# A hybrid DeltaNet and S5 layer: S5 setup, gate sums and chunk decays placed differently

## The chip, the cores and the metric

One core of one Trainium2 chip runs the program. The metric is the device time of that core in microseconds (us), the median of several executions. The engines are TensorE (PE in the rows, its weight load PEld), VectorE (DVE), ScalarE (ACT), GpSimd (POOL) and SyncE (SP, which here only issues DMAs). TensorE accumulates in PSUM; everything else lives in SBUF or in DRAM.

## What is computed

One layer of a streaming encoder: 4096 prompt frames and 32 sample frames of width 1024 go through an RMSNorm and one input projection. Its columns feed a gated DeltaNet (4 heads of 128) and an S5 state-space group (32 groups of 16 channels), each with a SiLU gate path; both outputs are joined, projected and added to x, and a last RMSNorm follows. Cut to what matters here:

```
q, k, v = silu(causal_conv4(h @ W_qkv));  q = l2norm(q) / sqrt(128);  k = l2norm(k)
beta = sigmoid(b);  g = -exp(A_log) * softplus(a + dt_bias);  gc = cumsum(g) in a block
decay = tril(exp(gc_i - gc_j))
lower = strict_tril((beta k) @ k.T * decay) + I
u = lower^-1 (beta v);  w = lower^-1 (beta k exp(gc));  attn = tril(q @ k.T * decay)
v_new = u - w @ S
o = (q * exp(gc)) @ S + attn @ v_new
S = S * exp(gc_last) + (k * exp(gc_last - gc)).T @ v_new
o_dn = rms_norm(o) * silu(z_dn)
S5: x_t = Lbar x_{t-1} + Bbar u_t;  y = Re(C x_t) + D u_t;  gy = gelu(y)
o_s5 = gy * sigmoid(gy @ glu_w + glu_b) * silu(z_s5)
x_new = x + concat(o_dn, o_s5) @ W_out;  y = rms_norm(x_new)
```

## The kernel before

The order of the instructions of each engine is fixed when the program is built, by a planner with estimated durations; an engine runs its own list in order and waits at its head. Products that need precision are three fp16 products of split operands: `pair` and `split` write a high half (ScalarE) and a low half (VectorE or GpSimd), `mm3` multiplies them.

**Stage one** (`phase_a`, up to about 640 us) normalises x, projects u for the S5 blocks (`uproj`), runs the S5 blocks and fills TensorE with the gate projections (`zproj`). `prep0` and `wfull` bring the first input and weights; `s5_setup` (L594) then makes the constants: exponentials, sines and powers of a 128x16 tile by short VectorE instructions, the rotation tables `rc` and `rs_` by doubling (L791 to L803), the B, C and Toeplitz matrices. It runs after the first projections, in the stretch 62 to 184 us. `s5_block` ends each group with eight stores of gy (L911) on SP. `gates` (L919) makes the decay sums `gc` and beta of all 32 prompt chunks, stores gc, exp(gc) and beta to DRAM (L976, L979), and transposes two of them on TensorE. `phase_b1` follows: it loads gc back (`gcr`), and `table` (L1004) makes from it, chunk by chunk, the decay matrix `dm` and stores it.

**Stage two** (`phase_b`, 922 to about 2086 us) interleaves on TensorE one dense stream (the projections of q, k, v and the S5 gate output, L48 with tile `pp`) with four streams of chunks of 128 frames. `Drive` orders them: a stream that yields n comes back when TensorE's own reckoned time has gone on by 1.5 n, and the chunk with the lowest number goes first. There are 33 chunks: 32 of the prompt and one for the sample. Chunk k uses the tiles of stream k mod 4, so tiles named `br`, `gr`, `knT`, `vb`, `kn` of chunk k are used again by chunk k+4.

A chunk (`chunk`, L1453) first loads exp(gc) into `gr` and beta into `br` (both spread over all partitions). **Front:** k's rows are transposed and squared, the root `rk` of the square sum is taken (`rsqrt`, L125: a power on GpSimd, L129, then three VectorE steps, L130 to L132), `kn` = k·rk; `br` is multiplied by the decay `dm` on GpSimd (L1548), q by `gr` (L1550) and split; the products k kᵀ and k qᵀ follow, and `at` in the tile of `br` (L1560). **Inverse** (`inverse`, L1639): on one of two slots, blocks of 4, 8, 16, 32 and 64 are inverted in a chain TensorE to VectorE and back (L1681, L1696, L1700, L1714, L1728), with a final correction (L1742 to L1746); its result U lies in the tile of `br` too. **Tail:** in the order of the chunks, the state `S` is split into `sp`, R and `vn` are made, `po` gets q·exp(gc)·S and attn·v_new (six products a head in one PSUM tile), `pS` updates S (L1614). Then the squares of `po`, the root `ro`, the gate z and the output (L1630) follow, split into `m16` (in the tile of `dm`) and stored by GpSimd (L1636). `load_dm` brings the decay matrix of a later chunk on SP (L1449).

**The last part** (2086 to 2454 us) is the output projection (`out`).

Of the kernel before, what the change touches and what calls it, by code (L numbers as in the profile page):

```python
# [6 lines left out]
F32 = mybir.dt.float32  # L7
# [10 lines left out]
H = 4  # L18
# [61 lines left out]
class Trunk:  # L80
    def __init__(self, ctx, tc, io, T):
# [6 lines left out]
        self.ws, self.un, self.uz, self.marks = {}, {}, {}, []  # L88
# [6 lines left out]
        self.ones = self.pool(self.ones_pool, "a_one").tile([128, 128], F32, name="ones")  # L95
# [6 lines left out]
        nc.vector.tensor_copy(self.ident16, self.ident)  # L102
        self.h_d = [self.dram.tile([2, 1024, 1024], F16, name=f"h_d{b}") for b in range(T // 1024)]
# [130 lines left out]
    def phase_a(self):  # L234
# [26 lines left out]
        nc.gpsimd.memset(self.rowo, 1.0)  # L261
        with ExitStack() as sc:
# [6 lines left out]
            self.un["zd"] = self.wfull(stg, "zd", self.w_z, self.nw, [mk[i] for i in w0], [mk[i] for i in w1], name="xz")  # L269
# [19 lines left out]
        self.s5_setup(tb)  # L289
# [54 lines left out]

        self.gcr = {key: self.tbl.tile([128, 128], F32, name="gc" + key, bufs=1)[:n] for key, n in (("p", H * self.NC), ("s", H))}
        for key, t in self.gcr.items():
            nc.sync.dma_start(t, self.gc_d[key].rearrange("h c t -> (h c) t"))
        order = list(range(self.NC))
        order.insert(2 * SP, self.NC)
        with self.tc.high_priority(offset=-250):  # L350
            for ci in order:
                self.table(ci)
        self.phase_b1()
# [25 lines left out]
    def wload(self, pool, nm, k0, k1, name="xw"):  # L379
# [69 lines left out]
    def h_hl(self, x, p):  # L449
# [3 lines left out]
        nc.sync.dma_start(xn, x)  # L453
# [140 lines left out]
    def s5_setup(self, wt):  # L594
        tc, nc, io = self.tc, self.nc, self.io
# [8 lines left out]
        self.wo8 = wt.tile([128, G, 8, 16], F32, name="wo8")  # L604
        with ExitStack() as sc:
            st = self.pool(sc, "a_s", side="right")

            def t16(nm):
                return st.tile([128, 16], F32, name=nm)

# [1304 lines left out]
```

## Time and profile before

| | |
|---|---|
| median of 3 runs | 2460.18 us (2457.91 to 2461.07) |
| the profiled execution | 2456.1 us, span of the trace 2454.4 us |
| TensorE busy | 2080.0 us, 85% |
| VectorE, ScalarE, GpSimd busy | 1578.9, 1204.6, 892.4 us |

The trace is of one execution. A share of busy time is an average over stages with different limits, so the rows below are by stretch, by line and by wait. A wait is put down to the engine or DMA whose end came last.

### The profile page before, as it was taken

Reading aid. Unit: us, or ns where it says so; the run is one execution under the profiler, and the core shown is the slowest. Engines: PE = TensorE matmul, PEld = TensorE weight load, DVE = VectorE, ACT = ScalarE, POOL = GpSimd, SP = SyncE. Lnnn points to the kernel's source line nnn. Section 1 sums busy time; section 2 is a strip of 40 time slices with the busy share of each in tenths; the row PEclk is TensorE's granted clock in tenths of the full one; section 3 lists DMA queues with packets and bytes.
Section 4 is the critical chain, followed back from the end, with each engine's and each line's share of the span. In section 5 each row is a group of like instructions: output and inputs, shape, how many; then the busy total and the mean of one; then the engine's idle time right before and its main releaser. Section 6 shows DMA issues by size and latency. Waiting matters only on the chain.

```text
span 2454.4 us, 47429 instructions
## 1 busy us (share of the span) xinstructions
PE 2080.0 (85%) x18040; PEld 1491.3 (61%) x18040; DVE 1578.9 (64%) x3715; ACT 1204.6 (49%) x3518; POOL 892.4 (36%) x1057
## 2 busy tenths in 40 slices
PE   3968898967799996986988789888878866999998
PEld 2635676734576554875777677777677743554443
DVE  3885766756474224886888778887878786642222
ACT  5457456423593113656666566666656564421101
POOL 1363011011102014556555555655655455420000
PEclk9989999979899997998999999999999888999999
DMA  5469877367864555231342233333333256455552
GB/s 164 152 165 248 164 164 183 67 75 104 233 174 125 116 123 112 57 80 40 79 83 69 62 66 85 76 83 76 62 58 58 58 143 123 117 142 155 152 146 90
DMA packets 458005, 278.05 MB, mean 113 GB/s; under 512 B 345112, under 2 KB 412928, under 8 KB 457264
## 3 DMA queue, kind: packets, MB, share of 16 engines
q1 hardware_dynamic: 435024, 206.94, 40.0%
q0 software_dynamic: 18000, 59.43, 7.3%
q10 hardware_dynamic: 4752, 8.65, 1.0%
q8 instruction: 141, 2.31, 0.4%
q14 instruction: 88, 0.72, 0.1%
HBM read 110.99 MB, written 86.23 MB: 80 GB/s over the span
## 4 chain that ended last, share of the span: by engine, by line
PE 32%; DVE 22%; DMA 15%; issue 14%; POOL 7%; ACT 6%; SPq 3%; POOLq 0%; DVEq 0%; ACTq 0%
PE pp L48 17%; PE pz L503 7%; DMA br<-be_d 6%; PE bk L48 4%; DVE acc L1354 3%; DMA gyt<-gy_d 2%; DMA h_d<-hl 2%; SPq L911 1%; DVE ubd L1687 1%; DMA gy_d<-vv 1%; DVE vv L879 1%; POOL br L1548 1%; PE bk L52 1%; PE pp L511 1%; DVE vv L885 1%
## 5 line engine op out<-in xcount | busy, mean ns | idle before, releaser
L503 PE MATMUL pz<-wz,hz 128*128 128x512 f16 (+1 forms) x1464 | 383.2, 388 | 20.3 <-DMA hz<-h_d 13.2
L1354 DVE SCALAR_TENSOR_TENSOR acc<-pp,cwu,acc 128x256 f32<-128x256 f32 x540 | 253.0, 475 | 39.1 <-ACT acc L1352 34.8
L48 PEld LDWEIGHTS <-mx 128*128 128x128 f16 (+1 forms) x1584 | 152.7, 98 | 178.8 <-issue 4.3
L503 PEld LDWEIGHTS <-hz 128*128 128x128 f16 (+1 forms) x1464 | 144.3, 100 | 179.2 <-issue 20.7
L48 PE MATMUL pp<-h,wk 128*128 128x259 f16 (+1 forms) x1632 | 224.6, 274 | 0.7 <-DVE gyt L1437 0.4
L48 PE MATMUL pp<-h,wv 128*128 128x259 f16 (+1 forms) x1632 | 220.3, 279 | 1.2 <-DVE acc L1354 1.2
L48 PE MATMUL pp<-h,wq 128*128 128x259 f16 (+1 forms) x1632 | 215.2, 275 | 1.3 <-DVE acc L1354 1.3
L511 PE MATMUL pp<-wa,ht 128*128 128x260 f16 x1536 | 189.8, 279 | 26.0 <-ACT wa L207 11.9
L48 PE MATMUL po<-wo,mx 128*128 128x512 f16 (+1 forms) x912 | 197.2, 379 | 0.3 <-ACT th L1184 0.3
L511 PEld LDWEIGHTS <-ht 128*128 128x128 f16 x1536 | 151.0, 100 | 52.8 <-issue 25.1
L48 PEld LDWEIGHTS <-wk 128*128 128x128 f16 x1632 | 155.1, 99 | 28.6 <-issue 3.6
L48 PEld LDWEIGHTS <-wv 128*128 128x128 f16 x1632 | 151.9, 101 | 33.4 <-issue 9.5
L48 PEld LDWEIGHTS <-wq 128*128 128x128 f16 x1632 | 151.6, 99 | 31.1 <-issue 9.5
L48 PE MATMUL pp<-wo,mx 128*128 128x512 f16 x672 | 153.9, 382 | 0.0
L537 POOL DMA_DIRECT2D z_d<-zt x64 | 36.7, 574 | 311.5 <-DVE zt L536 276.6
L48 PEld LDWEIGHTS <-a 128*128 128x128 f16 x1320 | 83.3, 102 | 89.1 <-issue 65.9
L536 DVE SCALAR_TENSOR_TENSOR zt<-zt,pz 128x512 f32<-128x512 f32 (+1 forms) x66 | 45.0, 682 | 134.7 <-ACT zt L535 134.5
L1522 ACT ACTIVATE jk<-bk 128x128 bf16<-128x128 f32 x396 | 109.9, 278 | 44.1 <-PE bk L52 32.5
L1548 POOL TENSOR_TENSOR br<-br,dm 128x512 f32<-128x512 f32 x33 | 42.4, 1284 | 196.9 <-DMA br<-be_d 137.0
L48 PE MATMUL pp<-wg,gh 128*128 128x512 f16 (+1 forms) x396 | 107.7, 403 | 6.0 <-DVE acc L1354 3.4
L1810 ACT ACTIVATE junk<-xt 128x1024 bf16<-128x1024 f32 (+1 forms) x19 | 20.1, 1056 | 176.4 <-issue 92.6
L1352 ACT ACTIVATE acc<-pp,cwu 128x256 f32<-128x256 f32 x180 | 85.1, 476 | 40.0 <-PE pp L48 26.9
(614 smaller groups left out, 4960.8 us busy)
## 6 DMA issues: line engine op xcount, KB each, us to landing
xn<-in_x SPq DMA_DIRECT2D x32, 512.0 KB, 6.0
h_d<-hl POOLq DMA_DIRECT2D x32, 512.0 KB, 5.2
z_d<-zt POOLq DMA_DIRECT2D x64, 256.0 KB, 3.7
xt<-in_x SPq DMA_DIRECT2D x18, 512.0 KB, 4.5
out_y<-xt SPq DMA_DIRECT2D x18, 512.0 KB, 3.6
dm_d<-tdm ACTq DMA_DIRECT2D x33, 256.0 KB, 3.2
dm<-dm_d SPq DMA_DIRECT2D x33, 256.0 KB, 2.8
gy_d<-vv SPq DMA_DIRECT2D x128, 64.0 KB, 2.3
```

What stands on the lines that cost most here:

```text
L48: return self.nc.tensor.matmul(out, lhs, rhs, start=start, stop=stop)
L52: return self.nc.tensor.transpose(out, src, ident)
L503: self.nc.tensor.matmul(ps, a[x][:, c], w[:, y, c], start=c == 0 and x == y == 0, stop=c == K - 1 and x == 1)
L511: self.nc.tensor.matmul(pu[hf][:, :260], ht[x][:, c, :m], self.w_a[:, y, c, 260 * hf:260 * hf + 260], start=c == 0 and x == y == 0, stop=c ...
L536: nc.vector.scalar_tensor_tensor(zt, zt, 1.0, pz, op0=ALU.add, op1=ALU.mult)
L537: nc.gpsimd.dma_start(rows(dst[0][blk]) if blk >= 0 else dst[1], zt)
L879: v.tensor_tensor(vv, vv, rs, op=ALU.mult)
L885: v.tensor_tensor_scan(*(t.rearrange("p a m -> p (a m)") for t in (vv[:, ri], rt, a[:, ri])), 0.0, op0=ALU.mult, op1=ALU.add)
L1352: nc.scalar.activation(acc, ps[:, 0:n], AF.Copy, scale=cw[:, e, 0:1])
L1354: v.scalar_tensor_tensor(acc, ps[:, j:j + n], cw[:, e, j:j + 1], acc, op0=ALU.mult, op1=ALU.add)
L1522: act.activation(junk, src[:, h], AF.Square, accum_out=out[:, h:h + 1])
L1548: gp.tensor_tensor(br, br, dm, op=ALU.mult)
```

## The change

- **Stage one.** `gates` keeps `gc` in the SBUF tile `gcr` from which `table` reads; it is no longer stored and loaded, and exp(gc) is neither made nor stored. exp(gc) per frame (`ngC` after an exponential) is made once after the tables. Stores of gy go out on GpSimd. `s5_setup` becomes a generator: its first part (constants, powers, rotation tables, with tiles in the space of `toep`) runs after the first inputs and weights have been prepared and ahead of the first projections; the rest runs where all of it stood. The loads of the gate weights wait for the fifth load of x.
- **Roots of a chunk.** `rsqrt4` makes the whole root on GpSimd: the power and four short steps, the last scaling folded in; the short sums beside it go to GpSimd as well.
- **Decays out of PSUM.** q is no longer multiplied by exp(gc) ahead of the product. `po` is made twice: first q·S, which ScalarE copies to `oa` (in the tile of `br`) with the factor exp(gc); then attn·v_new, which VectorE adds to `oa`. The output product reads `oa` from SBUF.
- **beta.** One tile `bl` holds beta of the next chunk; its load is issued on SP right after the multiply of the chunk before.
- **Inverse.** `a32` is made on GpSimd, `affine_select` acts on `br` before L1560, two selections go to ScalarE; the correction `e` is made on TensorE, which adds `Tf` and minus the identity into the same PSUM tile.
- `m16` uses the tile of `knT`. q's SiLU is made by ScalarE's own function, as for k and v, with one scaling per block of q.

```diff
+    def rsqrt4(self, x, tag, f):
+        gp = self.nc.gpsimd
...
+        gp.tensor_tensor(y, x, self.mhalf, op=ALU.pow)
+        gp.tensor_tensor(t, y, y, op=ALU.mult)
+        gp.tensor_tensor(t, t, x, op=ALU.mult)
+        gp.tensor_scalar(t, t, -3.0, -0.5 * f if isinstance(f, float) else f, op0=ALU.add, op1=ALU.mult)
+        gp.tensor_tensor(y, y, t, op=ALU.mult)
+        return y
@@ phase_a @@
+        setup = self.s5_setup(tb)
...
             hts += [self.prep0(s) for s in range(1, 8)]
...
-            self.un["zd"] = self.wfull(stg, "zd", self.w_z, self.nw, ..., name="xz")
+            self.un["zd"] = self.wfull(stg, "zd", self.w_z, self.nw, ..., name="xz", mark=self.xloads[4])
+            next(setup)
...
-        self.s5_setup(tb)
+        assert next(setup, None) is None
...
-        self.gcr = {key: self.tbl.tile(...) ...}
-        for key, t in self.gcr.items():
-            nc.sync.dma_start(t, self.gc_d[key].rearrange("h c t -> (h c) t"))
...
+        gcf = self.ngC.rearrange("t h c -> t (h c)")
+        self.last_exp = nc.scalar.activation(gcf, gcf, AF.Exp, scale=-1.0)
@@ s5_block @@
-                nc.sync.dma_start(gy[s], gn[16 * s:16 * s + 16, :, :128])
+                gp.dma_start(gy[s], gn[16 * s:16 * s + 16, :, :128])
@@ gates @@
-                gc = gp.tile([128, 128], F32, name="gc")[:p]
+                gc = self.gcr[key]
...
-                nc.scalar.activation(x, gc, AF.Exp)
-                nc.gpsimd.dma_start(self.eg_d[key].rearrange("h c t -> (h c) t"), x)
...
-                for t, dr, col in ((gc, self.gc_d, self.gcC), (hb, self.be_d, self.hbC)):
-                    nc.gpsimd.dma_start(dr[key].rearrange("h c t -> (h c) t"), t)
+                nc.gpsimd.dma_start(self.be_d[key].rearrange("h c t -> (h c) t"), hb)
+                for t, col in ((gc, self.gcC), (hb, self.hbC)):
@@ qkv @@
-                if b and nm != "q":
+                if b:
                     self.after(nc.scalar.activation(dst[:, h], acc, AF.Silu), self.last_exp)
...
+                    if b and nm == "q":
+                        nc.scalar.activation(dst, dst, AF.Copy, scale=self.sq["p"])
+    def load_be(self, ci):
+        self.bl = self.ck.tile([128, H, 128], F32, name="bl")
+        src = self.be_d["p"][:, ci] if ci < self.NC else self.be_d["s"][:, 0]
+        self.nc.sync.dma_start(self.bl, src.partition_broadcast(128))
@@ chunk @@
-        gr = t4("gr")
-        nc.sync.dma_start(gr, self.eg_d[key][:, cd].partition_broadcast(128))
         br = t4("br")
         dm = self.dms.pop(ci)
-        nc.sync.dma_start(br, self.be_d[key][:, cd].partition_broadcast(128))
...
-        rk = self.rsqrt(sk[:, 0], 128, H, "k")
+        rk = self.rsqrt4(sk[:, 0], "k", 1.0)
...
-        gp.tensor_tensor(br, br, dm, op=ALU.mult)
-        t = tmp()
-        gp.tensor_tensor(t[:, :, :m], qT[:, :, ts], gr[:, :, :m], op=ALU.mult)
-        qe = pair(gr, t)
+        gp.tensor_tensor(br, self.bl, dm, op=ALU.mult)
+        i = self.order.index(ci) + 1
+        if i < len(self.order):
+            self.load_be(self.order[i])
+        gp.affine_select(out=br, in_=br, ..., compare_op=ALU.not_equal, fill=0.0, base=0, channel_multiplier=-1)
...
-        v.tensor_scalar(sk[:, 1], sk[:, 1], self.eq[key], self.tau[key], op0=ALU.add, op1=ALU.mult)
+        gp.tensor_scalar(sk[:, 1], sk[:, 1], self.eq[key], self.tau[key], op0=ALU.add, op1=ALU.mult)
...
+        po = bk(self.po)
+        for h in range(H):
+            mm3(po[:, h], at_(qp, h), at_(sp, h))
         vn = pair(t4("knT"), pvn, v)
+        oa = t4("br")
+        for h in range(H):
+            act.activation(oa[:, h], po[:, h], AF.Copy, scale=self.ngC[:, h, ci:ci + 1])
         yield 2000
         po = bk(self.po)
         for h in range(H):
-            mm3(po[:, h], at_(qe, h), at_(sp, h), stop=False)
-            mm3(po[:, h], at_(aT, h), at_(vn, h), start=False)
+            mm3(po[:, h], at_(aT, h), at_(vn, h))
...
+        v.tensor_tensor(oa, oa, po, op=ALU.add)
-        squares(po, so)
-        v.scalar_tensor_tensor(so, so, 1.0 / 128, sk[:, 1], op0=ALU.mult, op1=ALU.add)
-        ro = self.rsqrt(so, 128, H, "o")
-        v.tensor_scalar(ro, ro, self.sdn, None, op0=ALU.mult)
+        squares(oa, so)
+        gp.tensor_tensor(so, so, sk[:, 1], op=ALU.add)
+        ro = self.rsqrt4(so, "o", self.hdn)
...
-            v.scalar_tensor_tensor(o[:, h], po[:m, h], ro[:m, h:h + 1], zc[:m, h], op0=ALU.mult, op1=ALU.mult)
+            v.scalar_tensor_tensor(o[:, h], oa[:m, h], ro[:m, h:h + 1], zc[:m, h], op0=ALU.mult, op1=ALU.mult)
...
-        m16 = dm.rearrange(...)
+        m16 = t4("knT").rearrange(...)
@@ inverse @@
-        v.tensor_tensor(a32, at, hb(self.bd32), op=ALU.mult)
-        gp.affine_select(out=at, in_=at, ..., compare_op=ALU.not_equal, fill=1.0, base=0, channel_multiplier=-1)
+        gp.tensor_tensor(a32, at, hb(self.bd32), op=ALU.mult)
...
-        v.tensor_scalar(T64[:, :, 32:64], T, self.rsel[:, 1:2], None, op0=ALU.mult)
+        act.activation(T64[:, :, 32:64], T, AF.Copy, scale=self.rsel[:, 1:2])
...
-        v.tensor_scalar(Tf[:, :, 64:128], T64, self.rsel[:, 3:4], None, op0=ALU.mult)
+        act.activation(Tf[:, :, 64:128], T64, AF.Copy, scale=self.rsel[:, 3:4])
...
-            pe.mm(p[:, h], al[:, h], Tf[:, h], start=False, stop=True)
-        e = t4("br")
-        v.scalar_tensor_tensor(e, p, -1.0, hb(self.ident), op0=ALU.mult, op1=ALU.add)
+            pe.mm(p[:, h], al[:, h], Tf[:, h], start=False, stop=False)
+            pe.mm(p[:, h], ident16, Tf[:, h], start=False, stop=False)
+            pe.mm(p[:, h], ident16, self.nid16, start=False, stop=True)
         eh = i4("a4")
-        act.copy(eh, e)
+        act.activation(eh, p, AF.Copy, scale=-1.0)
         el = i4("a32")
-        gp.tensor_tensor(el, e, eh, op=ALU.subtract)
+        v.scalar_tensor_tensor(el, p, -1.0, eh, op0=ALU.mult, op1=ALU.subtract)
```

## Rows read from the trace of the kernel before

**Rows 1.** Stretches: length; PE, PEld, DVE, ACT, POOL busy (x); clock; DMA

```profile
0.00:62.00 62.00, 22.17 (x192) 18.04 (x192) 20.18 (x55) 32.53 (x73) 8.49 (x26) 0.94 0.52 162
62.00:184.00 122.00, 98.12 (x656) 61.31 (x657) 102.92 (x348) 58.58 (x128) 59.27 (x81) 0.90 0.55 159
62.00:640.00 578.00, 463.84 (x3700) 336.47 (x3701) 388.94 (x910) 289.48 (x819) 133.45 (x208) 0.91 0.72 153
982.00:1964.00 982.00, 833.01 (x9275) 709.93 (x9273) 794.10 (x1953) 598.84 (x1906) 560.88 (x586) 0.94 0.31 68
```

**Rows 2.** Waits, whole run: us in all, times, longest us

```profile
POOL br L1548 <- DMA br<-be_d: 137.0, 21, 9.8
...
DVE rqt_k L130 <- POOL rq_k L129: 90.7, 26, 6.2
...
POOL br L1548 <- PE bk L48: 31.5, 6, 8.6
```

**Rows 3.** Timeline of GpSimd, 1500 to 1506 us: start, us, instruction

```profile
1500.47 1.27 POOL L1548 TENSOR_TENSOR br<-br,dm 128x512 f32<-128x512 f32 x1 [5.15 <-DMA br<-be_d]
...
1502.53 0.22 POOL L1525 TENSOR_SCALAR sk<-sk 128x4 f32<-128x4 f32 x1
...
1504.85 1.14 POOL L1483 TENSOR_TENSOR sp<-S_p,sp 128x512 f16<-128x512 f32 x1
```

**Rows 4.** The chain that ended last, by line (part 4 of the page)

```profile
PE pp L48 17%; PE pz L503 7%; DMA br<-be_d 6%; PE bk L48 4%; DVE acc L1354 3%; DMA gyt<-gy_d 2%; DMA h_d<-hl 2%; SPq L911 1%; DVE ubd L1687 1%; DMA gy_d<-vv 1%; DVE vv L879 1%; POOL br L1548 1%; PE bk L52 1%; PE pp L511 1%; DVE vv L885 1%
```

**Rows 5.** Waits of the whole run, TensorE's for the inverse

```profile
PE bk L48 <- DVE T L1681: 30.1, 27, 5.8
PE bk L48 <- DVE T L1700: 29.9, 17, 4.8
...
PE bk L48 <- DVE p L1696: 21.9, 19, 2.9
```

**Rows 6.** VectorE by line and form, 980 to 1964: busy, mean ns

```profile
L1354 DVE SCALAR_TENSOR_TENSOR acc<-pp,cwu,acc 128x256 f32<-128x256 f32 x483 | 225.6, 475 | 18.8 <-ACT acc L1352 15.6
...
L1360 DVE SCALAR_TENSOR_TENSOR qT<-th,acc 128x256 f32<-128x256 f32 x56 | 44.0, 809 | 17.0 <-PE bk L48 8.5 <-PE bk L52 7.2 <-ACT th L1359 1.3
...
L1630 DVE SCALAR_TENSOR_TENSOR kn<-bk,rq_o,vb 128x128 f32<-128x128 f32 x100 | 27.9, 339 | 0.2
...
L1714 DVE TENSOR_SCALAR T<-T,rsel 128x128 f16<-128x128 f16 x28 | 20.7, 740 | 0.0
...
L1560 DVE SCALAR_TENSOR_TENSOR br<-bk,br 128x512 f32<-128x512 f32 x28 | 19.2, 685 | 7.1 <-PE bk L48 6.9
...
L131 DVE TENSOR_TENSOR rqt_k<-rqt_k,sk 128x4 f32<-128x4 f32 x27 | 5.1, 187 | 0.1
```

**Rows 7.** Timeline of TensorE, 1484 to 1490 us

```profile
1485.64 0.83 PE L48 MATMUL bk<-tp,knT 128*128 128x128 f16 x12
```

**Rows 8.** ScalarE's groups by line and form, whole run

```profile
L1538 ACT ACTIVATE vb<-bk,hbC 128x128 f32<-128x128 f32 x132 | 37.8, 371 | 8.2 <-PE bk L52 7.0 <-DVE bk L1497 1.2
```

**Rows 9.** Waits of SP, 980 to 1964 us

```profile
SPq L1449 <- DMA mx_d<-dm: 244.3, 23, 22.2
```

**Rows 10.** Timeline of TensorE, 596 to 632 us

```profile
623.58 5.96 PE L1012 MATMUL pt<-gcp,ident 128*128 128x128 f32 x32 [22.63 <-DMA gcp<-gc_d]
```

**Rows 11.** Timeline of VectorE, 616 to 617 us

```profile
616.46 0.15 DVE L138 TENSOR_SCALAR am_g<-am_g 128x1 f32<-128x1 f32 x1 [22.06 <-POOL am_g L144]
```

**Rows 12.** VectorE's groups by line, 62 to 184 us

```profile
L800 DVE TENSOR_TENSOR rt<-rot_s,rot_c 128x256 f32<-128x256 f32 (+4 forms) x11 | 5.6, 505 | 0.0
...
L799 DVE TENSOR_TENSOR rot_c<-rot_c 128x256 f32<-128x256 f32 (+4 forms) x11 | 3.6, 347 | 0.0
...
L163 DVE SCALAR_TENSOR_TENSOR ea_s<-ea_s,er_s 128x16 f32<-128x16 f32 x15 | 2.6, 174 | 0.1
```

**Rows 13.** The costliest groups (part 5 of the page)

```profile
L537 POOL DMA_DIRECT2D z_d<-zt x64 | 36.7, 574 | 311.5 <-DVE zt L536 276.6
```

**Rows 14.** Waits of the whole run, TensorE's for the state

```profile
PE bk L48 <- ACT sp L1482: 12.7, 5, 3.9
```

More of the change, by code (lines that the diff above doesn't have):

```diff
@@ L94, in __init__ @@
         self.ones_pool = ExitStack()
-        self.ones = self.pool(self.ones_pool, "a_one").tile([128, 128], F32, name="ones")
+        one = self.pool(self.ones_pool, "a_one")
+        self.ones = one.tile([128, 128], F32, name="ones")
+        self.gcr = {key: one.tile([128, 128], F32, name="gc" + key)[:n] for key, n in (("p", H * T // 128), ("s", H))}
         nc.gpsimd.memset(self.ones, 1.0)
@@ L604, in s5_setup, with tile @@
         self.wo8 = wt.tile([128, G, 8, 16], F32, name="wo8")
+        left, made = [self.toep.rearrange("p x g n -> p (x g n)").bitcast(F32), 0], {}
+        class Room:
+            def tile(_, shape, dt, name):
+                if name not in made:
+                    n = 1
+                    for k in shape[1:]:
+                        n *= k
+                    t = left[0][:, left[1]:left[1] + n]
+                    left[1] += n
+                    made[name] = t.rearrange("p (a k) -> p a k", a=shape[1]) if len(shape) == 3 else t
+                return made[name]
@@ new lines, in s5_setup, with t16 @@
+        st = Room()
+        def t16(nm):
+            return st.tile([128, 16], F32, name=nm)
+        are, aim, ldt = t16("are"), t16("aim"), t16("ldt")
+        for t, nm in ((are, "A_re"), (aim, "A_im"), (ldt, "log_dt")):
+            nc.sync.dma_start(t, io["s5_" + nm])
+        dt, xr, xi, mag, sn, cs = (t16(n) for n in ("dt", "xr", "xi", "mag", "sn", "cs"))
+        v.tensor_single_scalar(are, are, -1e-4, op=ALU.min)
+        self.exp(dt, ldt, 128, 16, st, "s")
+        v.tensor_tensor(xr, are, dt, op=ALU.mult)
@@ L605, in s5_setup @@
+        for t in (self.rc, self.rs_):
+            nc.gpsimd.tensor_copy(t[:, :, 129:], t[:, :, :TS // 8 + 1])
+        yield
         with ExitStack() as sc:
             st = self.pool(sc, "a_s", side="right")
-            def t16(nm):
-                return st.tile([128, 16], F32, name=nm)
-            are, aim, ldt = t16("are"), t16("aim"), t16("ldt")
             bre = st.tile([128, 16, 16], F32, name="bre")
@@ L670, in s5_setup @@
-            qr = st.tile([128, 16, 8], F32, name="pwqr")
-            qi = st.tile([128, 16, 8], F32, name="pwqi")
-            for s in range(8):
-                v.tensor_copy(qr[:, :, s], pr[:, :, 7 - s])
-                nc.gpsimd.tensor_copy(qi[:, :, s], pi[:, :, 7 - s])
             br = st.tile([128, 16, 16], F32, name="bbr")
@@ L1137, in phase_b @@
         self.dms, self.sdone = {}, False
+        self.order = [i[0] for i in items]
+        self.load_be(self.order[0])
         for i in items[:NP]:
```

205 lines of the change are left out of this document (98 added, 107 removed).

## The prediction, made before the changed kernel ran

> **What bounds the kernel now.** I read the table by stretches first. TensorE is the engine to watch: in the long stage (982 to 1964 us) it is busy 833.0 of 982 us at a mean granted clock of 0.94, so 149 us are idle, and no other engine is fuller: VectorE 794.1, ScalarE 598.8, GpSimd 560.9 [rows 1]. Some 27 of the 33 chunks run in it (an instruction done once a chunk counts 27 or 28 there, as rows further down show), 36.4 us each, of which TensorE idles 149 / 27 = 5.5. In the stretch 62 to 640 TensorE lacks 578 − 463.8 = 114 us. The reader is to see that both stretches have an engine that wants to be full and isn't.
>
> The table of waits tells who makes the long stage wait. GpSimd's multiply of L1548 (`br*dm`) waited 137.0 us for the load of `br`, and VectorE waited 90.7 us in 26 places for GpSimd's `rq_k` [rows 2]. The two are one stall, as GpSimd's timeline shows: the multiply starts after 5.15 us of waiting for the load, and right behind it come the one of L1525 that opens the root of the keys of another chunk, and the split of the state `sp`, which is on the chain from chunk to chunk [rows 3]. The planner puts the multiply of chunk k+4 there because its tile `br` has just come free, a whole chunk before that product is needed; but the load into `br` can only start then, and everything behind it on GpSimd waits. The chain that ended last says the same: the load of `br` is 6% of the span, 147 us [rows 4]. The rest of the idle time of TensorE is VectorE's inverse: L1681, L1700 and L1696 were waited for 30.1 + 29.9 + 21.9 = 81.9 us [rows 5].
>
> **The long stage, part by part.** *The load.* It now goes into one tile `bl` one chunk ahead, so GpSimd finds it there. Of the 137.0 us, 90.7 were handed on to VectorE [rows 2], and VectorE is what TensorE waits for; the others fell on work that had time. I take **−91**, with bounds 0 (the wait only changes its name) and −137 (GpSimd's order is the whole chain). The load of `gr` and the tables behind it go too; I cost that at nothing, as no row shows a wait for it.
>
> *VectorE.* Twelve small or short groups of a chunk go to ScalarE, GpSimd or away, from L1714 (20.7 us, x28) to L131 of `rqt_k` (5.1 us, x27) in the view by form; the twelve sum to 161.7 us, 6.0 a chunk [rows 6]. The closing product of q's SiLU (L1360, 809 ns, x4 in two chunks) goes too: 1.6. Added are `oa + po`, priced by L1560 at 0.69, and the output product L1630 (4 x 0.34), which now reads two SBUF tiles where it read PSUM and SBUF. The nearest pair for that is L1360 (two from SBUF, 809 ns) against L1354 (PSUM and SBUF, 475 ns) of one shape, a factor of 1.7; so up to 4 x 0.34 x 0.7 = 0.95. Net −6.0 of the 794.1 / 27 = 29.4 us that VectorE works in a chunk, or 20%. I let the waits of [rows 5] fall in that proportion: 0.20 x 81.9 = **−17**, bounds 0 and −82.
>
> Here a rule speaks against the change. The Trainium skill ("SBUF — State Buffer", section "SBUF: two separate sides") says that a VectorE instruction with both inputs in SBUF and a GpSimd instruction that reads SBUF shut each other out for their whole length. The trace agrees in so far as L1360 is the slow one of the pair; by the rule the 0.95 would arise only where GpSimd is met, and the term would be −17 to −20 rather than −17. What it would do to GpSimd is a rival below.
>
> *TensorE* gets eight 128x128 fp16 products a chunk (identity against `Tf`, and minus the identity), in place of an addition by VectorE. Twelve of such take 0.83 us [rows 7], eight 0.55, times 33 chunks: **+18** where TensorE is the bound, 0 where it idles; I take all of it.
>
> *GpSimd* loses three 128x512 operations a chunk (the q·gr product, its split, the split of `e`), at 1.14 as the `sp` row, 3.4 us. It gains the `a32` product at the same price, eight short ones of the two roots and two short sums at 0.22 [rows 3]: 1.1 + 2.2 = 3.3. That is no change; the powers themselves stay. The roots no longer go to VectorE and back, but the short ones now stand in GpSimd's order: nothing either way. `affine_select` moves forward onto `br`, off the way between VectorE and the inverse: nothing.
>
> *ScalarE* gains the copies of `po` (4 x 0.371, [rows 8]), two selections (one such and at most two) and half a scaling of q, 128x1024, at most 8 / 2 = 4 such pieces: up to 11 x 0.371 = 4.1 a chunk, less a cast that goes. Hidden: ScalarE is idle 38% of the stage, 14 us a chunk [rows 1]; without that cover it is 33 x 4.1 = 135.
>
> *New waits.* `po` is a single PSUM bank: the second product waits on TensorE until ScalarE has copied the first, and `pS` stands behind it, on which the next chunk's state waits. A yield of 2000 (3 us in the order's own time) is meant to cover four copies of 0.37. At nothing, with a rival below. On SP the load of `bl` stands behind `load_dm` (L1449), where SP waited up to 22.2 us for a store out of `dm` [rows 9]. It has a chunk, 36 us, and GpSimd waited at most 9.8 for such a load [rows 2]: it still fits. `m16` no longer uses `dm`, which frees that tile earlier. At nothing.
>
> *The clock.* 0.94 against full is worth 833 x 0.06 = 50 us at most [rows 1]. It falls where TensorE idles; if two thirds of the idle time goes, I expect half back: **−24**, bounds 0 and −50.
>
> **The first stage.** *Decay sums on chip.* TensorE waited 22.63 us for `gcp` to come back from DRAM, until 623.58 [rows 10]. But VectorE stood for `am_g` until 616.46, and the work after that (the negated sums, which the tables need) comes only then [rows 11]. So the gain is 623.6 − 616.5 = **−7**, bounds 0 and −22.6.
>
> *S5 setup early.* Six table groups of 11, L800 (5.6) to L799 (3.6), sum to 26.4 us; with them go some 146 short ones at the 0.174 of L163, 25 us [rows 12]. They leave 62 to 184, where VectorE is busy 102.9 of 122 and TensorE idles 24 [rows 1]. With half of VectorE's work gone I take −15 of these 24. At the start VectorE idles 62 − 20 = 42 of 62 us, in which they mostly fit, but VectorE works in order and the splits of the first weights may stand behind them: I take +10, bounds 0 and +51. Net **−5**.
>
> *gy stores by GpSimd.* 128 of them at 0.574 [rows 13] are 73 us on an engine busy 133 of 578 [rows 1]. They stand before the stores of h and z in its order; SP loses as many issues and the waits before them. Bounds −17 (a quarter of the 67 us of idle TensorE that the two items above leave in 62 to 640) and +73 (each in the path). I take 0.
>
> **The sum.** −91 − 17 + 18 − 24 − 7 − 5 = −126 against the profiled run of 2456.1: 2330. The median of the runs shown is 4.1 above that run: 2334. I forecast **2334 us**.
>
> Its own ends: the load at −137, VectorE −17, TensorE +18, clock −40, first stage −29 (gc −14, setup −15) make −205, so 2255; the load at −55, VectorE −5, TensorE +18, clock −12, first stage +12 make −42, so 2418.
>
> **The rivals.** (1) *The stall takes another form.* `br` now also holds `oa`, until the output product at the end of the chunk, later than before, and the planner can put the multiply of k+4 in front of that again. For it: GpSimd also waited 31.5 us for TensorE to free `br` [rows 2]. Against it: the planner puts it where it believes the tile is free, and a wait for VectorE's product has no load of up to 9.8 us behind it. The load and the clock then bring nothing: 2460 − 17 + 18 − 12 = 2449. Chance 0.10. (2) *Slower: TensorE stands for the drain of `po`.* If ScalarE, busier by up to 4.1 a chunk, reaches its four copies 4 us after their cover, TensorE, `pS` and the state chain wait 4 us in each of 33 chunks: 132. The nearest wait is TensorE's for ScalarE's `sp`, 12.7 us in 5, at most 3.9 [rows 14]. That size in every chunk would make 2334 + 132 = 2466; it decides where the lag past the cover is above 126 / 33 = 3.8, from where the change is slower than no change. Against it: only 5 such waits in 33 chunks now. Chance 0.05. (3) *Nothing but TensorE is left.* 5.5 x 33 = 182 us of idle go and the clock gives 40: 2460 + 18 − 182 − 40 − 12 = 2244. Chance 0.05. (4) *GpSimd is held by VectorE.* If the output product, 4 x 0.58, keeps GpSimd out each chunk and all of it reaches the chain, 33 x 2.3 = 76 is added: 2410. This is the skill's lock named above. In the trace GpSimd has 421 us without work in the long stage to take it up. Chance 0.05.
>
> **How the numbers follow.** The forecast holds 0.75. The range goes from 2255 to 2415: it takes in (4) and the forecast's ends and leaves out (1), (2) and (3), together 0.20. About 0.2%, 5 us, is what a measurement of this kernel can tell from no change. Faster: 0.75 + 0.05 + 0.05 + 0.06 of (1) = 0.91. Same: 0.03 of (1). Slower: (2) and the tail of (1), 0.06.
>
> **What would show it.** In the profile after, GpSimd's L1548 waits for a load below 20 us in all and VectorE's for `rq_k` below 20; VectorE some 130 to 160 us less busy in the long stage, TensorE 18 more; idle time of TensorE there near 50 to 60 and the clock at 0.97; the first `gc` transposes at about 616 and not 623.6; the first u matmuls not later than before by more than 10. I am wrong if GpSimd still waits some 100 us in L1548 under another name, if TensorE waits over 50 us for the copies out of `po`, or if the u matmuls start 20 us later.

## The result and the profile after

The changed kernel takes 2354.82 us (median of 4, 2353.89 to 2355.19) where the kernel before takes 2460.41 in the same comparison: a ratio of 0.9571, interval 0.9559 to 0.9583, or 106 us less. The forecast was 2334 in 2255 to 2415. The direction and the main mechanism held; two terms of the sum were wrong by 47 and 33 us in opposite directions, and one edit that was costed at nothing is worth some 15 to 30.

The same stretches as in [rows 1], with the long stage at its new place (busy us by engine, granted clock, DMA share, GB/s):

```profile
0.00:62.00 62.00, 31.09 (x256) 24.78 (x257) 28.79 (x166) 30.81 (x73) 10.18 (x30) 0.97 0.62 186
62.00:184.00 122.00, 92.84 (x587) 54.38 (x586) 90.39 (x230) 57.21 (x119) 55.27 (x73) 0.87 0.45 132
62.00:640.00 578.00, 475.45 (x3708) 338.21 (x3707) 380.87 (x788) 293.12 (x824) 194.12 (x325) 0.91 0.74 151
960.00:1900.00 940.00, 853.24 (x9853) 737.26 (x9854) 702.19 (x1686) 668.46 (x2152) 589.08 (x835) 0.96 0.29 68
```

The long stage is shorter by about 42 us in this cut, TensorE fuller (853 of 940 against 833 of 982) and its clock 0.96 for 0.94. The waits that answer [rows 2, 5] (whole run: us, times, longest; L1716 and L1735 are the L1681 and L1700 of before):

```profile
POOL br L1581 <- DVE kn L1667: 21.4, 21, 2.0
ACT kn L1562 <- POOL rq_k L137: 21.4, 18, 10.6
...
PE bk L48 <- DVE T L1716: 17.2, 18, 3.8
...
PE bk L52 <- ACT kn L1562: 12.1, 6, 5.6
...
POOL br L1581 <- DMA bl<-be_d: 11.6, 2, 6.3
...
PE bk L48 <- DVE T L1735: 9.0, 12, 1.5
...
PE bk L48 <- ACT br L1642: 8.5, 10, 1.6
```

The multiply (now L1581) waits 11.6 us for a load instead of 137.0, and VectorE has no part in the key root any more, for which ScalarE's `kn` now waits 21.4 us. The load has left the chain that ended last, where it was 6% of the span [rows 4]:

```profile
PE pp L48 23%; PE pz L522 9%; PE bk L48 7%; DMA gyt<-gy_d 3%; PE bk L52 2%; DVE acc L1384 2%; ACT jk L1555 2%; DMA dm_d<-tdm 1%; PE pt L1047 1%; DMA hz<-h_d 1%; DVE kn L1667 1%; DMA ab_d<-abt 1%; SPq L1349 1%; ACT acc L1382 1%; ACT br L1642 1%
```

To see where the 106 us come from, cut the run at three marks: the first squares of a chunk, the first and the last update of the state. A view of one line gives the start of its first and last instruction. For the kernel before and the changed one (duration min/median/max, first and last start):

```profile
L1614 DVE SCALAR_TENSOR_TENSOR S_p<-S_p,egl,bk x128: 274/342/350, 1034.0 to 2216.5; 128x128 f32<-128x128 f32 x128
L1522 ACT ACTIVATE jk<-bk x396: 250/278/339, 931.3 to 2216.2; 128x128 bf16<-128x128 f32 x198
```

```profile
L1651 DVE SCALAR_TENSOR_TENSOR S_p<-S_p,egl,bk x128: 333/340/348, 1042.4 to 2111.6; 128x128 f32<-128x128 f32 x128
L1555 ACT ACTIVATE jk<-bk x264: 250/278/362, 925.2 to 2038.9; 128x128 bf16<-128x128 f32 x132
```

| kernel (marks in us) | ratio to before | first squares | from there to the first update | first to last update | after that |
|---|---|---|---|---|---|
| before | 1 | 931.3 | 102.7 | 1182.5 | 237.9 |
| changed | 0.9571 | 925.2 | 117.2 | 1069.2 | 241.2 |
| e1 order only | 0.9722 | 928.1 | 99.6 | 1105.0 | 244.6 |
| e2 load in br | 0.9847 | 924.9 | 107.6 | 1142.5 | 238.4 |
| e3 stage one only | 0.9976 | 919.4 | 98.3 | 1193.6 | 231.9 |
| e4 first four | 0.9629 | 945.0 | 102.0 | 1076.1 | 234.9 |
| e5 gy on SP | 0.9681 | 940.7 | 114.8 | 1075.6 | 238.9 |
| e6 setup late | 0.9554 | 918.6 | 116.2 | 1073.0 | 234.7 |
| e7 e on VectorE | 0.9592 | 919.6 | 116.0 | 1086.6 | 221.3 |
| e8 roots on VectorE | 0.9485 | 916.8 | 115.6 | 1056.0 | 239.1 |
| e9 gy on GpSimd only | 0.9869 | 907.1 | 100.2 | 1169.7 | 237.7 |
| e10 a32 on VectorE | 0.9607 | 921.2 | 117.0 | 1078.7 | 234.7 |
| e11 three taken back | 0.9539 | 925.4 | 114.7 | 1060.5 | 239.1 |
| e12 key root on VectorE | 0.9505 | 920.3 | 112.7 | 1055.2 | 238.9 |

So the change won 6 us up to the first squares, lost 14.5 at the start of the chunks, won 113 among them and lost 3 behind. These two executions are 101.6 us apart. Ratios are to the kernel before on the same chip, where it took 2450 to 2460 us; a gain in us below is the ratio times 2460. Marks are of one profiled execution each, and they scatter. The kernel before, e9 and e3 run the same code for the chunks and take 1182.5, 1169.7 and 1193.6 us there: in e9 another first stage made the planner order them differently, and e3, in the order of before, is still 11 us longer. The changed kernel, e5 and e6 differ by 6. A difference of such a size in one stretch isn't put down to an edit by the marks alone, and a ratio holds what the planner's new order did along with the edit.

### The profile page after: what moved, and what is told of

It is laid out like the page before. It is cut to its first block, busy times and chain, and to the rows that moved or that the text cites. A ratio compares the mean times of both kernels' runs of the same rounds, so it can differ in the third digit from the quotient of the medians.

```text
span 2352.8 us, 47799 instructions
## 1 busy us (share of the span) xinstructions
PE 2068.0 (88%) x18304; PEld 1492.9 (63%) x18304; DVE 1440.2 (61%) x3289; ACT 1251.0 (53%) x3695; POOL 959.4 (41%) x1444
## 4 chain that ended last, share of the span: by engine, by line
PE 43%; issue 11%; ACT 7%; DMA 7%; DVE 6%; POOL 4%; SPq 1%; DVEq 0%; POOLq 0%; ACTq 0%
PE pp L48 23%; PE pz L522 9%; PE bk L48 7%; DMA gyt<-gy_d 3%; PE bk L52 2%; DVE acc L1384 2%; ACT jk L1555 2%; DMA dm_d<-tdm 1%; PE pt L1047 1%; DMA hz<-h_d 1%; DVE kn L1667 1%; DMA ab_d<-abt 1%; SPq L1349 1%; ACT acc L1382 1%; ACT br L1642 1%
## 5 line engine op out<-in xcount | busy, mean ns | idle before, releaser
L530 PE MATMUL pp<-wa,ht 128*128 128x260 f16 x1536 | 196.3, 284 | 27.1 <-ACT wa L222 10.4
L48 PE MATMUL pp<-h,wv 128*128 128x259 f16 (+1 forms) x1632 | 209.9, 272 | 1.0 <-DVE acc L1384 1.0
L555 DVE SCALAR_TENSOR_TENSOR zt<-zt,pz 128x512 f32<-128x512 f32 (+1 forms) x66 | 44.9, 680 | 102.0 <-ACT zt L554 101.3
L48 PEld LDWEIGHTS <-a 128*128 128x128 f16 x1320 | 78.2, 98 | 37.3 <-issue 28.3
L1844 DVE SCALAR_TENSOR_TENSOR xt<-po,uo,xt 128x512 f32<-128x512 f32 (+1 forms) x38 | 28.5, 749 | 116.7 <-PE po L48 116.6
L948 POOL DMA_DIRECT2D gy_d<-vv x128 | 67.7, 535 | 78.7 <-ACT vv L943 40.3
```

What stands on the lines that cost most here:

```text
L48: return self.nc.tensor.matmul(out, lhs, rhs, start=start, stop=stop)
L530: self.nc.tensor.matmul(pu[hf][:, :260], ht[x][:, c, :m], self.w_a[:, y, c, 260 * hf:260 * hf + 260], start=c == 0 and x == y == 0, stop=c ...
L555: nc.vector.scalar_tensor_tensor(zt, zt, 1.0, pz, op0=ALU.add, op1=ALU.mult)
L948: gp.dma_start(gy[s], gn[16 * s:16 * s + 16, :, :128])
L1844: v.scalar_tensor_tensor(xt[:m, sl], ps, self.uo[:m], xt[:m, sl], op0=ALU.mult, op1=ALU.add)
```

## The experiments

**Is it the load?** e1 takes the kernel before and adds one ordering edge, so that the multiply cannot stand ahead of its own chunk's front:

```diff
-        gp.tensor_tensor(t, kn, col(self.ed), op=ALU.mult)
+        mark = gp.tensor_tensor(t, kn, col(self.ed), op=ALU.mult)
         kd = pair(kn, t)
-        gp.tensor_tensor(br, br, dm, op=ALU.mult)
+        self.after(gp.tensor_tensor(br, br, dm, op=ALU.mult), mark)
```

> The kernel before with one ordering edge and nothing else: on GpSimd the multiply br*dm may not stand ahead of the multiply of kn by the decay in its own chunk. The load of beta then has most of a chunk to land before it is asked for. Theory A (the long stage lost its time because that multiply stood a chunk too early in GpSimd's list, with the key root and the state split behind it): the wait for br falls from 137 us to under 15, VectorE's for rq_k from 91 to under 25, time about 2460 - 91 = 2370. Theory B (VectorE's load is what holds TensorE, and the stall only filled time in which GpSimd had nothing due): 2445 to 2460, the wait for rq_k is replaced by TensorE's waits for the inverse.

2379.8 us, ratio 0.9722 (0.9691 to 0.9754): 68 us less, interval 61 to 76. No other operation was changed. VectorE's wait for the key root and TensorE's for the inverse (90.7 and 81.9 before, [rows 2, 5]) become:

```profile
PE bk L48 <- DVE T L1681: 18.9, 18, 5.0
...
PE bk L48 <- DVE T L1700: 13.1, 11, 5.1
...
PE bk L48 <- DVE p L1696: 5.6, 8, 1.3
...
DVE rqt_k L130 <- POOL rq_k L129: 4.8, 9, 1.0
```

The multiply itself (L1548) waits for its load once in the run, 0.5 us instead of 137.0.

Between the first update and the end of the projections, by stretch (the kernel before, e1, the changed kernel):

```profile
1034.00:1983.00 949.00, 797.26 (x8870) 678.61 (x8868) 769.72 (x1909) 576.43 (x1837) 546.40 (x569) 0.94 0.32 70
```

```profile
1028.00:1902.00 874.00, 781.73 (x8907) 666.28 (x8905) 770.07 (x1914) 578.68 (x1848) 552.30 (x574) 0.96 0.32 77
```

```profile
1042.00:1896.00 854.00, 777.79 (x9094) 675.76 (x9094) 646.82 (x1566) 614.79 (x1984) 548.55 (x784) 0.97 0.29 68
```

TensorE's idle time falls from 949 − 797.3 = 151.7 us to 874 − 781.7 = 92.3 by the one edge, and its work, the same in both, from 797.3 to 781.7 with the clock at 0.96 for 0.94. The order of GpSimd's list, then, was worth 59 us of idle time and 16 of clock in this stretch. Theory A stands, at about three quarters of its size (68 of 91).

e2 does the reverse: all of the change but the early load, with beta loaded into `br` as before.

```diff
         br = t4("br")
+        nc.sync.dma_start(br, self.be_d[key][:, ci if key == "p" else 0].partition_broadcast(128))
...
-        gp.tensor_tensor(br, self.bl, dm, op=ALU.mult)
-        i = self.order.index(ci) + 1
-        if i < len(self.order):
-            self.load_be(self.order[i])
+        gp.tensor_tensor(br, br, dm, op=ALU.mult)
```

> The changed kernel, except that beta is loaded into the tile br of each chunk as before, without the shared tile and its early load. As br now also holds the scaled first product until the output is made, the load can start only later than before. Theory A: the multiply waits for the load again, 100 us or more in all, and most of the gain of the long stage goes: 2430 to 2455. Theory B: VectorE stays relieved, 2355 to 2375.

2411.9 us, ratio 0.9847 (0.9815 to 0.9878), 38 us less than before, where theory A had asked for 2430 to 2455. The stall is there in full, and longer than the 137.0 us of before:

```profile
POOL br L1581 <- DMA br<-be_d: 169.7, 30, 8.4
```

The two parts add up: 68 (e1) + 38 (e2) = 106, the whole change. So the load is worth 68, put into the kernel before or taken out of the changed one, and neither theory had room for the 38 of the rest.

**The first stage.** e3 puts its edits alone into the kernel before (early setup, decay sums in SBUF, gy stores by GpSimd, as in the diff).

> The kernel before with the edits of the first stage alone (early S5 setup with its delayed weight loads, decay sums kept in SBUF, gy stores by GpSimd); the chunks are as before. Theory A, by the times at which the first chunk's squares begin (931.3 before, 925.2 after): about 6 us less, 2454. If the first stage gave the 29 us by which the decay tables start earlier: 2431. If its gy stores cost more than the rest brings: above 2462.

2445.0 us, 0.9976 (0.9959 to 0.9993): 6 us less. Its own first squares come 12 us earlier than before (919.4), and its chunks take 11 longer between the updates. e9 takes one of its edits:

```diff
-                nc.sync.dma_start(gy[s], gn[16 * s:16 * s + 16, :, :128])
+                gp.dma_start(gy[s], gn[16 * s:16 * s + 16, :, :128])
```

> The kernel before with one edit: the 128 stores of gy are issued by GpSimd instead of SP. Theory A (the forecast): within 3 us of the kernel before. Theory B (they are what the first stage gained: with them on SP in the changed kernel the first squares of a chunk came at 940.7 us, with them on GpSimd at 917 to 925): 10 to 20 us less, more than the three edits of the first stage together (6), so that the other two cost.

2419.4 us, 0.9869 (0.9844 to 0.9894): 32 us less, 24 of them by the first squares. e5 takes the same line back in the changed kernel:

```diff
-                gp.dma_start(gy[s], gn[16 * s:16 * s + 16, :, :128])
+                nc.sync.dma_start(gy[s], gn[16 * s:16 * s + 16, :, :128])
```

> The changed kernel with the 128 stores of gy issued by SP again. Theory A (the stores cost nothing on either queue, as forecast): 0.9571 of the kernel before, within 3 us of the changed kernel. Rival B (on GpSimd they stand ahead of the stores of h and z, whose loads TensorE waited for, 25.5 us against 13.2 before): about 10 us less. Rival C (on SP they hold up the loads of h, xn and z): 10 us more.

0.9681 (0.9645 to 0.9717), 27 us slower than the changed kernel by the ratios; 15 of them stand at the first squares. In both directions the step that was costed at nothing is the one that pays in the first stage. The stretch 184 to 640 in the kernel before and in e9:

```profile
184.00:640.00 456.00, 365.72 (x3046) 275.16 (x3045) 286.02 (x562) 230.90 (x692) 74.18 (x127) 0.92 0.77 152
```

```profile
184.00:640.00 456.00, 387.62 (x3201) 285.85 (x3200) 295.54 (x579) 240.10 (x713) 147.13 (x258) 0.94 0.82 159
```

TensorE gets 22 us more work done in the same 456 us, GpSimd is busy 73 us longer, as worked out, and had the time. The stores wait for ScalarE's gelu; on SP the loads stood behind that wait, 51.8 us in 10 places:

```profile
SPq L911 <- ACT vv L906: 51.8, 10, 14.9
```

In e9 that wait is gone from SP and stands on GpSimd, 42.1 us in 9 places. Which loads came earlier by it was not traced.

e6 puts the S5 setup back to its old place.

```diff
-            next(setup)
...
+        next(setup)
         assert next(setup, None) is None
```

> The changed kernel with the S5 setup wholly at its old place (the delayed weight loads stay). Theory A, by the forecast (15 gained in 62 to 184 us, 10 paid at the start): 5 us more than the changed kernel. Rival B: the setup early is worth the whole 24 us that TensorE idled in 62 to 184, then 15 to 24 more. Rival C: the saturated stretch from 660 us on starts no earlier because the gate projections wait for h, then within 2 us.

0.9554 (0.9535 to 0.9573), which overlaps with the 0.9571 of the changed kernel. But it doesn't test the setup: the edit moved its place in the program, and the planner still ran it early: VectorE has 166 instructions up to 62 us in both, where the kernel before has 55 [rows 1]. The rotation tables of the kernel before, the changed one and e6 (first and last start):

```profile
L799 DVE TENSOR_TENSOR rot_c<-rot_c x11: 191/414/425, 118.1 to 145.1; 128x256 f32<-128x256 f32 x7, 128x16 f32<-128x16 f32 x1, 128x32 f32<-128x32 f32 x1, 128x64 f32<-128x64 f32 x1
```

```profile
L716 DVE TENSOR_TENSOR rot_c<-rot_c x11: 190/414/1078, 86.8 to 126.1; 128x256 f32<-128x256 f32 x7, 128x16 f32<-128x16 f32 x1, 128x32 f32<-128x32 f32 x1, 128x64 f32<-128x64 f32 x1
```

```profile
L715 DVE TENSOR_TENSOR rot_c<-rot_c x11: 192/419/1078, 86.0 to 125.1; 128x256 f32<-128x256 f32 x7, 128x16 f32<-128x16 f32 x1, 128x32 f32<-128x32 f32 x1, 128x64 f32<-128x64 f32 x1
```

So what the early setup is worth stays open. By [rows 1] and the rows after, the first stage's edits moved work from one stretch to the next: TensorE did 9 us more by 62 us and 5 less in the 122 after; whether the setup or the later weight loads did it, no run tells. What e6 shows is how far a new order alone moves the kernel: 4 us in all, 6.6 at the first squares. The decay sums weren't run alone. Of the 26 us between e3 and e9, 12 are there at the first squares and belong to the setup, the sums and the later weight loads together; which of them costs them stays open. The rest lies among chunks of the same code.

**The start of the chunks.** It took 14.5 us longer. With the single tile `bl` SP brings the loads of the first chunks one by one, each after the multiply of the one before and behind the transposing loads of h (SP's timeline: start, duration):

```profile
924.57 0.37 SPq L1481 DMA_DIRECT2D bl<-be_d  x1
...
936.77 0.52 SPq L1481 DMA_DIRECT2D bl<-be_d  x1
937.38 9.21 SPq L1349 DMA_TRANSPOSE h<-h_d  x1
...
951.53 0.52 SPq L1481 DMA_DIRECT2D bl<-be_d  x1
...
962.08 0.36 SPq L1481 DMA_DIRECT2D bl<-be_d  x1
971.12 0.33 SPq L1481 DMA_DIRECT2D bl<-bes_d  x1
```

The five loads go out from 924.6 to 971.1 us. e4 loads beta of the first four chunks straight into their own `br` tiles, at once, and keeps `bl` from the fifth on.

```diff
-        self.load_be(self.order[0])
+        self.load_be(self.order[NP])
+        for p, i in enumerate(items[:NP]):
+            self.br0[i[0]] = t = self.ck.tile([128, H, 128], F32, name=f"br{p}")
+            nc.sync.dma_start(t, self.be_d["p"][:, i[0]].partition_broadcast(128))
```

> The changed kernel, but the first four chunks load beta into their own br tiles ahead of the stage, all at once, and the shared tile is loaded ahead for the fifth. If the single shared tile makes the start of the long stage a chain of load, multiply, load (the first state update came 117.5 us after the first squares, 103.1 before), those 14 us come back: about 2341, with the multiply's wait for the load near 0. If the start is late for another reason (ScalarE's copies, GpSimd's longer list): 2350 to 2355.

0.9629 (0.9601 to 0.9658): nothing gained, rather 0.6 points lost. The stretch from the first squares to the first update is back at 102.0 us, as expected, but the first squares come at 945.0, 20 us later: in this order of ScalarE's list they stand behind a store of the gate projections (waits of 905 to 965 us).

```profile
ACT jk L1560 <- DMA z5s_d<-zt: 15.1, 1, 15.1
```

So short-cutting the chain this way gives nothing. What it costs, the table tells: the stretch from the first squares to the first update takes 113 to 117 us in the eight kernels that start with the single tile and 98 to 108 in the six that don't. In e2, whose first squares come with those of the changed kernel (924.9), the first update comes 9.9 us earlier. So the chain is worth about 10 of the 14.5 us; the rest was not traced.

**What the rest is made of.** e7 undoes the part of the correction: the identity products off TensorE, the sum on VectorE, the diagonal set in the inverse.

```diff
-            pe.mm(p[:, h], ident16, Tf[:, h], start=False, stop=False)
-            pe.mm(p[:, h], ident16, self.nid16, start=False, stop=True)
+        e = t4("br")
+        v.scalar_tensor_tensor(e, p, -1.0, hb(self.ident), op0=ALU.mult, op1=ALU.add)
```

> The changed kernel with the correction of the inverse as before: no identity products on TensorE, the sum with the identity on VectorE, its low half on GpSimd, and the unit diagonal set by GpSimd inside the inverse. By the forecast's terms: TensorE 18 us less, VectorE 33 x 0.68 = 22 us busier, of which a fifth or so shows: 10 us less than the changed kernel. Rival: TensorE idles enough in the long stage (76 us) that the 18 us were free, while GpSimd's step inside the inverse (58.9 us of waiting before) lengthens it: 5 to 20 us more.

0.9592 (0.9566 to 0.9617): no difference that the intervals can tell. It's 5 us more, give or take 7. In the whole run TensorE is busy 2056.9 us for 2068.0, so the identity products are 11 us of its work and not the 18 that the sum had charged. VectorE is busy 2 us more only, since it makes `e` in place of `el` (L1781 in the changed kernel); the engine that the change relieved is GpSimd, 959.4 for 991.9. What each of these is worth by itself the run doesn't tell; together they come to nothing that shows.

e8 takes the roots back: the power on GpSimd, the other steps on VectorE, as before the change.

```diff
-        rk = self.rsqrt4(sk[:, 0], "k", 1.0)
+        rk = self.rsqrt(sk[:, 0], 128, H, "k")
...
-        ro = self.rsqrt4(so, "o", self.hdn)
+        ro = self.rsqrt(so, 128, H, "o")
+        v.tensor_scalar(ro, ro, self.hdn, -2.0, op0=ALU.mult, op1=ALU.mult)
```

> The changed kernel with the roots of the chunks as before: the power on GpSimd, the three steps after it on VectorE, and the scaling of the output root there too. Theory A (VectorE's load sets the inverse's pace): the roots are 3.3 of the 6.0 us that it lost in a chunk, so half of the forecast's -17 is lost, 8 to 10 us more than the changed kernel. Rival B (the hops between the engines matter, and VectorE stands in order for GpSimd's key root as before, 90.7 us): 25 to 60 more. Rival C (GpSimd's list is the tighter one now, 589 us busy of 940): 5 to 10 less.

2323.6 us, 0.9485 (0.9465 to 0.9506): faster than the changed kernel by 0.9 points, 21 us. So the roots on GpSimd cost time, although they took 43 us off VectorE's work (busy 1440.2 us in the whole run with them, 1483.3 without), 1.3 a chunk. Rival C alone had the sign. Some 8 of the 21 us stand at the first squares already (916.8 for 925.2), ahead of any root of a chunk, and aren't the roots'; 13 lie between the updates, where e5 and e6, with the roots on GpSimd, take longer still (1075.6 and 1073.0 for 1056.0). e12 keeps the output root on GpSimd and takes only the key root back (the first two lines of that diff).

> The changed kernel with the key root's steps on VectorE and the output root still on GpSimd. With both on VectorE the long stage lost 21 us. Theory A (the key root's four steps on GpSimd delay kn, which ScalarE waited for 21.4 us, and it opens the front): most of the 21 come from here, 0.949 to 0.952 of the kernel before. Theory B (it is the length of GpSimd's list, whichever root is on it): half of it, 0.953. Theory C (the output root, behind which the split of the state stands): 0.956 to 0.958, no gain.

2330.4 us, 0.9505 (0.9483 to 0.9527): 16 of the 21, and between the updates, 1055.2, all that e8 gains there. GpSimd's timeline in the changed kernel shows what the root becomes there:

```profile
1426.98 1.04 POOL L133 TENSOR_TENSOR rq_k<-sk,mhalf 128x4 f32<-128x4 f32 x1
1428.39 0.20 POOL L1660 TENSOR_TENSOR so<-so,sk 128x4 f32<-128x4 f32 x1 [0.37 <-ACT jk L1555]
1428.54 0.20 POOL L134 TENSOR_TENSOR rqt_k<-rq_k 128x4 f32<-128x4 f32 x1
1428.70 1.01 POOL L133 TENSOR_TENSOR rq_o<-so,mhalf 128x4 f32<-128x4 f32 x1
1429.68 0.20 POOL L135 TENSOR_TENSOR rqt_k<-rqt_k,sk 128x4 f32<-128x4 f32 x1
1429.82 0.61 POOL L1793 COPY br<-uf 128x512 f16<-128x512 f16 x1
1430.40 0.36 POOL L134 TENSOR_TENSOR rqt_o<-rq_o 128x4 f32<-128x4 f32 x1
1430.73 0.20 POOL L136 TENSOR_SCALAR rqt_k<-rqt_k 128x4 f32<-128x4 f32 x1
...
1431.04 0.20 POOL L137 TENSOR_TENSOR rq_k<-rq_k,rqt_k 128x4 f32<-128x4 f32 x1
```

The power is done at 1428.02; the four steps after it, 0.2 us each, end at 1431.24, because the output root's power (1.01), a copy (0.61) and that root's own steps stand between them. On ScalarE `kn` waits for it, and TensorE for `kn` 12.1 us in 6 places; in e12:

```profile
PE bk L52 <- ACT kn L1562: 3.4, 5, 1.8
```

That is 9 us less. It's no proof that the root was the cause: with the roots on VectorE the same wait was 14.0 us before the change and 10.5 in e1. The rest of the 16 was not traced to a wait. The place in GpSimd's list is the likely cause, then, and not a shown one.

e10 takes `a32` back to VectorE.

```diff
-        gp.tensor_tensor(a32, at, hb(self.bd32), op=ALU.mult)
+        v.tensor_tensor(a32, at, hb(self.bd32), op=ALU.mult)
```

> The changed kernel with a32 made by VectorE again. In the changed kernel VectorE's a4 takes 1193 ns instead of 722 and GpSimd's a32 1387, as both start from the same product and read SBUF at the same time. Theory A (the two shut each other out, so that moving a32 saved VectorE only 0.25 us a chunk and cost GpSimd 1.39): a4 is back at 0.72, and the time falls by 5 to 15 us. Theory B (GpSimd has room, and VectorE's 0.25 us and the earlier end count): 0 to 8 us more.

0.9607 (0.9588 to 0.9626), 9 us more: theory B's sign, though a new order alone moves as much. `a4` is back at 0.73 us, as theory A said, but `a32` takes 1.11 on VectorE and not the 0.72 of before: in 14 of its 15 slow places GpSimd makes `al` (L1695) beside it (VectorE by line and form, 960 to 1860 us):

```profile
L1691 DVE TENSOR_TENSOR a<-br,bd 128x512 f16<-128x512 f32 x28 | 31.0, 1109 | 0.0
...
L1689 DVE TENSOR_TENSOR a<-br,bd 128x512 f16<-128x512 f32 x28 | 20.4, 730 | 0.3
```

e11 puts e6, e8 and e10 together.

> The changed kernel with three of its moves taken back: both roots and a32 on VectorE, the S5 setup at its old place. If the gains add: 0.9485 (roots) less 4 us of the setup and 5 to 15 of a32, so 0.941 to 0.946 of the kernel before, about 2308 to 2320. If VectorE becomes the bound of the inverse again with 0.25 + 2.3 us more in a chunk: 0.950 or more.

0.9539 (0.9521 to 0.9558), 13 us worse than e8 alone and in the second branch of its expectation. As e6's edit left the setup where it ran, e11 is e8 and e10 together. That VectorE bounds the inverse again fits, but wasn't traced. None of e7, e8 and e10 holds the gain of the rest: the moves that were not taken back alone (q's decay out of PSUM, the selections and q's SiLU on ScalarE, the tile of `m16`) stay unseparated. The best version of these runs is e8, 2323.6 us, which beats both kernels.

## Why the prediction came out as it did

**The mechanism was right.** The stall of L1548 stood in GpSimd's order, was handed to VectorE by the key root, and was worth more than everything else. e1 shows it with one edge. Rival (1), that the stall only changes its name, is out: the multiply waits 21.4 us for the output product in the place of 137.0, in waits of at most 2.0. Of the signs, the load's wait came as forecast (11.6 us, below 20); TensorE's idle time stayed at 76 us where 50 to 60 were forecast, and VectorE worked 123 us less from the first update to the end of the projections, where 130 to 160 were.

**That the number came so near is in part luck.** The terms below are off by +47, −33 and +6 us; they add up to the 20 by which 2334 was too low.

**The load and the clock were too large: −115 forecast (−91 and −24), −68 measured** in e1 (61 to 76), which holds both. The step that failed is "90.7 were handed on to VectorE, and VectorE is what TensorE waits for". A wait of VectorE is not a wait of TensorE: e1 took 86 us off the one and 59 off TensorE's idle time in the long stretch. In e1, TensorE's three waits for the inverse fall from 81.9 to 37.6 us without any relief of VectorE, so much of [rows 5] was the same stall seen from TensorE, and I counted it a second time as the base of VectorE's term. The clock gave 16 in the long stretch where I had 24.

**The relief was too small: −17 + 18 = +1 forecast, about −32 measured** (38 in e2 less 6 of the first stage in e3). The +18 is 11 us of TensorE's work in e7, and nothing of it shows in the time; by e8 the relief would have been worth some 13 to 21 more with the roots left where they were. Which moves made the −32, no run tells. "Nothing either way" for the roots on GpSimd is the step that failed: I named GpSimd's order and put it at nothing without a row. The work is equal, but in that order a step of 0.2 us waits behind what the planner puts between.

**The first stage: −12 forecast, −6 measured, for other reasons.** The gy stores, costed at 0 with bounds −17 and +73, brought 24 at the first squares (e9; 15 in e5); the bound of gain was too narrow, since it went by TensorE's idle time and not by the wait on SP that stood in the view of waits. The setup's −5 no run shows, and its premise failed: the tables were to leave the stretch 62 to 184 and run there from 86.8 us on, and VectorE's work in it fell from 102.9 us to 90.4 only. Whether the −7 of the decay sums came, no run tells either: the 22.63 us for `gcp` [rows 10] went, and the first transposes of gc began at 594.5 us, earlier than forecast, but the tables then stood for the store of a table that did not land, and TensorE with them (the waits of 594 to 640 us); why it landed late stays open:

```profile
DVE tdm L1049 <- DMA dm_d<-tdm: 22.1, 1, 22.1
...
PE pt L1047 <- DVE tdm L1049: 16.3, 1, 16.3
```

**The start of the chunks: not in the sum, +14.5.** I had held that the load of `bl` has a chunk's time to land. It has, from the fifth on; at the start four fronts come at once, and the chain costs about 10. These us lie inside the −68 and the −32, not beside them.

**The other rivals.** (2) TensorE's waits for the copies out of `po` are 8.5 us in all: the cover holds. (3) TensorE alone: 76 us of idle time remain in the long stretch. (4) GpSimd and VectorE do hold each other (last section); the output product takes 454 ns a piece where [rows 6] had 339, and the price is inside the −32:

```profile
L1667 DVE SCALAR_TENSOR_TENSOR kn<-br,rq_o,vb 128x128 f32<-128x128 f32 x100 | 39.4, 454 | 5.5 <-POOL rq_o L137 5.1
```

## What to carry to other kernels

Ask of every long wait of an in-order engine whether the instruction that waits is due at all: one ordering edge gave two thirds of this change. When a wait is traced through a second engine to the one that bounds, price it by what the bounding engine idles, once, and not by the waits of both. Before short dependent steps are moved to another engine, look at what its list will put between them; work that is equal in sum can be late in order. Where a planner orders the instructions, look in the trace whether an edit moved anything (e6's did not), before its time is read as an answer.

## What the hardware showed

VectorE's `a4` and GpSimd's `a32`, which start from the same product and both read two tiles in SBUF, shut each other out. Here VectorE began first, and then GpSimd, 0.09 us ahead (two places in the changed kernel, VectorE's and GpSimd's timelines):

```profile
1059.27 0.69 DVE L1689 TENSOR_TENSOR a<-br,bd 128x512 f16<-128x512 f32 x1
1059.31 1.67 POOL L1691 TENSOR_TENSOR a<-br,bd 128x512 f16<-128x512 f32 x1 [2.40 <-DVE br L1592]
```

```profile
1281.28 1.61 DVE L1689 TENSOR_TENSOR a<-br,bd 128x512 f16<-128x512 f32 x1
1281.19 1.16 POOL L1691 TENSOR_TENSOR a<-br,bd 128x512 f16<-128x512 f32 x1 [3.78 <-DVE br L1592]
```

First `a4` takes 0.69 us and `a32` 1.67; then `a32` 1.16 and `a4` 1.61. Whichever starts second pays. In 28 of the 33 chunks the two overlap by more than 0.1 us, and in each of these `a32` ends 1.01 to 1.03 us after an earlier `a4`, or `a4` 0.54 to 0.56 us after an earlier `a32`, however much of the first was left when the second began. That is the exclusion that the Trainium skill states ("SBUF — State Buffer", "SBUF: two separate sides"). Moving `a32` to GpSimd saved VectorE little: `a4` takes 1.19 us in the mean, where before it and `a32` took 0.72 each. In the kernel before, `a4` was longer than 0.8 us in 2 of 33 places, both beside an instruction of GpSimd; its median was 0.69 us:

```profile
L1652 DVE TENSOR_TENSOR a<-br,bd x33: 678/686/1666, 951.1 to 2127.7; 128x512 f16<-128x512 f32 x33
```

GpSimd's next step, L1656, waited for the two products there, 66.1 us in 19 places.
